# Attention scores of a query block in one PSUM tile: a change to the softmax stage of a two-layer hybrid trunk

## Chip, core and metric

The kernel runs on one core of one Trainium2 chip. The metric is the device time of one execution in microseconds (us). Engines are called PE (TensorE matmuls; PEld its weight loads), DVE (VectorE), ACT (ScalarE), POOL (GpSimd) and SP (SyncE, which issues most DMAs).

## What is computed

The program computes a trunk of two layers over 256 context and 1024 latent tokens (1280 keys) at model width 1024: an S5 state-space mixer with a SwiGLU FFN, then multi-head latent attention with a second FFN. The change lies in the attention alone, which per head is

```
def softmax_attend(q, k, v):
    s = jnp.einsum('bqhd,bkhd->bhqk', q, k).astype(jnp.float32) * (MLA_QK ** -0.5)
    p = jax.nn.softmax(s, axis=-1)
    return jnp.einsum('bhqk,bkhd->bqhd', p.astype(v.dtype), v)
```

There are 16 heads, the queries are the 1024 latent tokens, the keys and values are all 1280 tokens. Work is fp32 throughout: operands are split into a high and a low fp32r part, and a score product is the sum of three matmuls (low by high, high by low, high by high).

## The kernel before

The attention stage is the stretch of `trunk` from the pool `ps4` (L1658) on. A **unit** is one head and one half (512) of the queries; there are 32 (L1684). A unit has four **blocks** of 128 queries and ten **key tiles** of 128 keys.

- `scores_a` (L1697) makes the scores of a block against the first 1024 keys: six matmuls into a two-bank PSUM tile `psS`, of which there are two buffers (L1701), and a `reduce_max` on DVE (L1708).
- `scores_b` (L1711) adds the last 256 keys: three matmuls into the one-bank tile `psE` (one buffer, L1717), a second `reduce_max` on DVE, a DVE `scalar_tensor_tensor` that joins both maxima and scales them by `nsc` (L1722), and two exponentials on ACT, of 256 and of 1024 columns, with the row sums into `rs2` (L1725, L1726). The result is `p`, 128 queries by 1280 keys in SBUF.
- `key_tile` (L1729) transposes four 128x128 pieces of `p` (four blocks, one key tile) on PE into the one-bank tile `psT` (two buffers) and splits the result. For key tiles 1, 4, 6 and 9 (`DIRECT`, L1788) ACT copies PSUM to `ph` and DVE subtracts that from PSUM to give `pl`. For the others ACT copies PSUM to `pf`, DVE casts `pf` to `ph`, and POOL subtracts to give `pl`.
- `pv` (L1763) multiplies a key tile with the values: two matmuls into `psO` (one buffer), and at the tenth a DVE multiplication by the reciprocal row sums.
- `row_sums` (L1747) adds the two halves of `rs2`, takes the reciprocal, transposes it on PE into a `psT` buffer, and sends it through DRAM to be spread over partitions.

The eight PSUM banks are 2x2 for `psS`, 1 for `psE`, 2 for `psT` and 1 for `psO`. The main loop (L1804 to L1830) runs over the units and their ten key tiles. In unit n it transposes and multiplies the `p` of unit n while it makes the scores of unit n+1, one block at key tiles 0, 2, 4 and 6 (`SCORES_AT`): `scores_a`, then `key_tile`, then `scores_b`. `pv` runs five key tiles behind (`LAG`). Before the loop the four blocks of unit 0 are made (the prologue, L1799 to L1802). The order in which each engine runs its instructions is a scheduler's, made from this text and the free buffers; each engine runs its own list in that order, and waits on counters of the other engines.

Of the kernel before, what the change touches and what calls it, by code (L numbers as in the profile page):

```python
# [34 lines left out]
TOK = CTX + SEQ  # L35
# [5 lines left out]
HEADS = 16  # L41
# [142 lines left out]
def trunk(tc, I, out, dbg=None):  # L184
# [20 lines left out]
    V, S, Q, T, D_ = (Engine(*e) for e in zip("VSQTD", (nc.vector, nc.scalar, nc.gpsimd, nc.tensor, nc.sync)))  # L205
# [14 lines left out]
    def copy(o, a):  # L220
        S.activation(o, a, AF.Copy)
# [18 lines left out]
    def pool(name, bufs=1, side="left", space=None):  # L240
        kw = {} if space is None else {"space": space}
        cm = tc.tile_pool(name=name, bufs=bufs, side=side, reuse_waits="tile", **kw)
        p = cm.__enter__()
        opened.append((p, cm))
        return p
# [15 lines left out]
    pp = None  # L261
# [4 lines left out]
    def psG():  # L266
        return psA(4)
# [101 lines left out]
    def const(name, w, p=cp):  # L369
        t = p.tile([128, w], F32, name=name)  # L370
        if p is cp:
            deferred.append((t, I[name]))
        else:
            dma(t, I[name])
        return t
# [7 lines left out]
    ident = const("ident", 128)  # L383
# [54 lines left out]
    def halves(t):  # L438
        return t.rearrange("p (n w) -> p n w", n=2)

    def psN():
        return psB(8).rearrange("p (n w) -> p n w", n=1)
# [90 lines left out]
    pp = pool("ps0", 4, space=PSUM)  # L533
# [607 lines left out]
    def tB():  # L1141
        return hB.tile([128, 2, 640], F32R, name="hb", tag="hb")
# [34 lines left out]
    pp = pool("ps1", 4, space=PSUM)  # L1177
    bgn = norm0_seven(s1, 0, h, psG)
    for c in range(2):
        av = []  # L1180
        for m in range(8):
# [10 lines left out]
            o = tB()  # L1192
# [24 lines left out]
        for m in range(8):  # L1217
            wt = ws.whole(8)
            pt = psG()
# [142 lines left out]
    pp = pool("ps2", 4, space=PSUM)  # L1362
# [4 lines left out]
    pp = ps3 = pool("ps3", 4, space=PSUM)  # L1367
# [5 lines left out]
    sc = pool("sc")  # L1373
    scq = sc.tile([128, 8, HEADS], F32, name="scq")
    nsc = sc.tile([128, 8, HEADS], F32, name="nsc")
# [257 lines left out]
    pp = pool("psq", 4, space=PSUM)  # L1633
# [24 lines left out]
    pp = pool("ps4", 2, space=PSUM)  # L1658
    hA = pool("hA1", 8)
    at = pool("at")  # L1660
    rs2 = at.tile([128, HEADS, 2, 2, 4], F32, name="rs2")
    kv = {}

    def tA1():
# [20 lines left out]
    qts = {}  # L1685
# [9 lines left out]
    open_s = []  # L1695

    def scores_a(n, b):  # L1697

        hd, hf = units[n]
        kt, qt = kv[hd][0], qts[n]  # L1700
        pa = pp.tile([128, 2, 512], F32, name="psS", tag="psS", bufs=2)  # L1701
        qs = slice(b * 128, b * 128 + 128)
        for j, (qp_, kp_) in enumerate(((1, 0), (0, 1), (0, 0))):
            for o, c0 in ((pa[:, 0], 0), (pa[:, 1], 512)):
                T.matmul(o, qt[:, qp_, qs], kt[:, kp_, c0:c0 + 512], start=j == 0, stop=j == 2)
        flat = pa.rearrange("p a b -> p (a b)")
        mx = at.tile([128, 3], F32, name="mx", bufs=4)
        V.reduce_max(mx[:, 0:1], flat, axis=AX.X)  # L1708
        open_s.append((n, b, flat, mx))

    def scores_b():  # L1711

        n, b, flat, mx = open_s.pop()
        hd, hf = units[n]
        kt, qt = kv[hd][0], qts[n]
        i = 4 * hf + b
        pb = pp.tile([128, 256], F32, name="psE", tag="psE", bufs=1)  # L1717
        qs = slice(b * 128, b * 128 + 128)
        for j, (qp_, kp_) in enumerate(((1, 0), (0, 1), (0, 0))):
            T.matmul(pb, qt[:, qp_, qs], kt[:, kp_, 1024:], start=j == 0, stop=j == 2)  # L1720
        V.reduce_max(mx[:, 1:2], pb, axis=AX.X)
        V.scalar_tensor_tensor(mx[:, 2:3], mx[:, 0:1], mx[:, 1:2], nsc[:, i, hd:hd + 1], op0=ALU.max, op1=ALU.mult)  # L1722
        sc = scq[:, i, hd:hd + 1]
        p = at.tile([128, TOK], F32, name="p", bufs=8)
        S.activation(p[:, 1024:], pb, AF.Exp, bias=mx[:, 2:3], scale=sc, accum_out=rs2[:, hd, hf, 1, b:b + 1])  # L1725
        S.activation(p[:, :1024], flat, AF.Exp, bias=mx[:, 2:3], scale=sc, accum_out=rs2[:, hd, hf, 0, b:b + 1])  # L1726
        return p

    def key_tile(ps, k):  # L1729
        tp = pp.tile([128, 512], F32, name="psT", tag="psT", bufs=2)  # L1730
        for b in range(4):
            T.transpose(tp[:, b * 128:b * 128 + 128], ps[b][:, k * 128:k * 128 + 128], ident)
        ph_ = at.tile([128, 512], F32R, name="ph", bufs=6)
        pl_ = at.tile([128, 512], F32R, name="pl", bufs=6)
        if k in DIRECT:
            copy(ph_, tp)
            sub(pl_, tp, ph_.bitcast(F32))
        else:
            pf = at.tile([128, 512], F32, name="pf", bufs=3)
            copy(pf, tp)  # L1740
            V.tensor_copy(ph_, pf)
            sub(pl_, pf, ph_.bitcast(F32), Q)
        return ph_, pl_
# [3 lines left out]
    def row_sums(n):  # L1747

        hd, hf = units[n]
        r4 = at.tile([128, 4], F32, name="r4", bufs=2)  # L1750
        add(r4, rs2[:, hd, hf, 0], rs2[:, hd, hf, 1])
        V.reciprocal(r4, r4)
        pt = pp.tile([128, 512], F32, name="psT", tag="psT", bufs=2)
        T.transpose(pt[0:4, 0:128], r4, ident)
        rt = at.tile([4, 128], F32, name="rt", bufs=2)
        V.tensor_copy(rt, pt[0:4, 0:128])
        dst = rsd[hd:hd + 1, hf * 512:hf * 512 + 512]
        dma(dst.rearrange("a (b p) -> (a b) p", b=4), rt)
        rb = wp.tile([128, 1024], F32, name="rb", tag="wr")
        dma(rb[:, 0:512], dst.to_broadcast([128, 512]))  # L1760
        rbs[n] = rb
# [37 lines left out]
    for b in range(4):  # L1799
        scores_a(0, b)  # L1800
        cur.append(scores_b())
    row_sums(0)  # L1802
    pend = []
    for n in range(NU):  # L1804
        hd, hf = units[n]
        nxt = []
        for k in range(10):
            if n + 1 < NU and k in SCORES_AT:
                scores_a(n + 1, SCORES_AT.index(k))
            if k == 1 and n + 2 < NU:  # L1810
                load_q(n + 2)
            if k == 1 and hf == 0 and hd + 1 < HEADS:
                load_kv(hd + 1)
            if k in (3, 8) and hf == 0 and hd + 1 < HEADS:
                split_k(hd + 1, k // 8)
            if k == 3 and hf == 1 and hd + 1 < HEADS:
                split_v(hd + 1)
            if k == 5 and n + 2 < NU:
                split_q(n + 2)
            if k == 5 and n % 4 == 1 and n > 4:  # L1820
                ot0.append(tA1())
                heads_in(at, n // 4 - 1, 0, ot0[-1])
            pend.append((n, k, key_tile(cur, k)))
            if open_s:
                nxt.append(scores_b())
            if k == 9 and n + 1 < NU:
                row_sums(n + 1)
            if len(pend) > LAG:
                pv(*pend.pop(0))
        cur = nxt  # L1830
# [7 lines left out]
    pp = pool("ps5", 8, space=PSUM)  # L1838
# [33 lines left out]
    for c, (ot, bg, rate) in enumerate(((ot0, second(), 1), (ot1, norm1(s1, 0, h), 2))):  # L1872
        for m in range(8):
# [3 lines left out]
            pt = psN()  # L1877
# [34 lines left out]
```

## Time and profile before

| | us |
|---|---|
| median of 3 runs | 3405.48 (3405.12 to 3406.26) |
| profiled execution | 3405.42 |
| its span, first to last instruction | 3403.6 |
| PE busy in the span | 3181.9 (93%) |
| DVE busy | 2760.2 (81%) |
| ACT busy | 1745.4 (51%) |
| POOL busy | 1032.8 (30%) |
| DVE maxima over psS, 128 of them | 155.6 |
| ACT exponentials over psS, 128 of them | 154.0 |

Busy time counts an instruction from its start to its end. Matmuls overlap, so PE's busy time is not the time that it needs. The granted clock is TensorE's, as a share of its full 2.4 GHz: 1.00, or 0.50 for 1.2 GHz; in a stretch that holds both it is between. "Idle before <- X" names the engine and the tile whose end released an instruction. All helper calls have the line L198, so tiles are told apart by name. The attention stage lies between about 1986 and 2597 us.

### The profile page before, as it was taken

Reading aid. Unit: us, or ns where it says so; the run is one execution under the profiler, and the core shown is the slowest. Engines: PE = TensorE matmul, PEld = TensorE weight load, DVE = VectorE, ACT = ScalarE, POOL = GpSimd, SP = SyncE. Lnnn points to the kernel's source line nnn. Section 1 sums busy time; section 2 is a strip of 40 time slices with the busy share of each in tenths; the row PEclk is TensorE's granted clock in tenths of the full one; section 3 lists DMA queues with packets and bytes.
Section 4 is the critical chain, followed back from the end, with each engine's and each line's share of the span. In section 5 each row is a group of like instructions: output and inputs, shape, how many; then the busy total and the mean of one; then the engine's idle time right before and its main releaser. Section 6 shows DMA issues by size and latency. Waiting matters only on the chain. (4 is left out here: it accounts for less than half of the span.)

```text
span 3403.6 us, 55331 instructions
## 1 busy us (share of the span) xinstructions
PE 3181.9 (93%) x20468; PEld 2922.9 (86%) x20468; DVE 2760.2 (81%) x4640; ACT 1745.4 (51%) x3218; POOL 1032.8 (30%) x812
## 2 busy tenths in 40 slices
PE   6977889999999999999999989899899899999999
PEld 5977789999999999999988767777777799889998
DVE  6878867878888998888867678888885788898887
ACT  5556652424333453344455557777775544454443
POOL 2456510101112121121334345555554421221111
PEclk8988899999999999999999999999999999999999
DMA  7579876552333323323426742222225333233232
GB/s 258 139 162 190 177 196 230 185 180 75 112 101 111 112 81 124 108 67 99 131 95 176 197 122 73 85 67 78 75 70 166 119 104 107 93 120 106 99 107 75
DMA packets 196384, 423.08 MB, mean 124 GB/s; under 512 B 22737, under 2 KB 73873, under 8 KB 195089
## 3 DMA queue, kind: packets, MB, share of 16 engines
q1 hardware_dynamic: 182288, 392.27, 36.1%
q0 software_dynamic: 13824, 27.27, 4.5%
q8 instruction: 162, 2.65, 0.3%
q14 instruction: 110, 0.89, 0.1%
HBM read 326.89 MB, written 53.49 MB: 112 GB/s over the span
## 5 line engine op out<-in xcount | busy, mean ns | idle before, releaser
L198 PE MATMUL psB<-hs,wb 128*128 128x320 f32 (+1 forms) x7392 | 1001.2, 297 | 26.3 <-DVE wb L198 18.6
L198 PEld LDWEIGHTS psB<-hs,wb 128*128 128x128 f32 x7392 | 989.7, 189 | 36.6 <-DVE wb L198 23.2
L198 ACT ACTIVATE wb<-wr 128x512 fp32r<-128x512 f32 (+3 forms) x704 | 404.4, 593 | 448.6 <-PE psB L198 227.6
L198 DVE TENSOR_TENSOR wb<-wr,wb 128x512 fp32r<-128x512 f32 (+3 forms) x704 | 491.9, 709 | 170.1 <-ACT wb L198 169.0
L198 PE MATMUL psB<-hb,wb 128*128 128x320 f32 (+1 forms) x3360 | 602.3, 340 | 12.5 <-ACT hb L198 6.4
L198 PEld LDWEIGHTS psB<-hb,wb 128*128 128x128 f32 x3360 | 544.7, 188 | 65.7 <-ACT hb L198 8.0
L198 POOL TENSOR_TENSOR ws<-wr 128x512 f32<-128x512 f32 x176 | 243.8, 1391 | 1151.4 <-DMA wr<-in_fi 606.0
L198 ACT ACTIVATE wb<-ws 128x512 fp32r<-128x512 f32 x352 | 218.9, 627 | 268.6 <-PE psB L198 195.3
L198 POOL TENSOR_TENSOR pl<-pf,ph 128x512 fp32r<-128x512 f32 x192 | 250.7, 1306 | 259.8 <-DVE ph L198 256.0
L198 DVE TENSOR_TENSOR wb<-ws,wb 128x512 fp32r<-128x512 f32 x352 | 273.8, 782 | 31.2 <-ACT wb L198 29.6
L198 PE MATMUL psA<-ha,wb 128*128 128x320 f32 x1680 | 249.9, 311 | 4.4 <-ACT ha L198 4.4
L198 PEld LDWEIGHTS psA<-ha,wb 128*128 128x128 f32 x1680 | 248.9, 189 | 5.0 <-ACT ha L198 4.6
L198 PE MATMUL psS<-kt,qt 128*128 128x512 f32 x768 | 213.1, 403 | 1.1 <-ACT p L198 1.1
L198 PEld LDWEIGHTS psT<-ident,p 128*128 128x128 f32 x1280 | 147.5, 140 | 72.6 <-issue 20.2
L198 PE MATMUL psT<-ident,p 128*128 128x128 f32 x1280 | 190.1, 275 | 20.3 <-DVE pl L198 17.3
L198 DVE TENSOR_REDUCE mx<-psS 128x1 f32<-128x1024 f32 x128 | 155.6, 1215 | 19.1 <-PE psS L198 18.6
L198 PEld LDWEIGHTS psS<-kt,qt 128*128 128x128 f32 x768 | 139.7, 189 | 29.2 <-ACT p L198 2.1
L198 POOL TENSOR_TENSOR acc<-acc,sq 128x640 f32<-128x640 f32 (+1 forms) x51 | 82.9, 1626 | 249.2 <-ACT sq L198 210.4
L198 ACT ACTIVATE p<-psS,mx,scq 128x1024 f32<-128x1024 f32 x128 | 154.0, 1203 | 0.0
L198 ACT ACTIVATE hb<-sg 128x640 fp32r<-128x640 f32 (+1 forms) x104 | 72.0, 693 | 147.8 <-DVE sg L198 147.4
L198 PE MATMUL psO<-ph,vt 128*128 128x512 f32 x320 | 139.7, 436 | 2.3 <-DVE ph L198 0.4
L198 DVE TENSOR_TENSOR ws<-ws,wr 128x512 f32<-128x512 f32 x88 | 89.2, 1014 | 60.3 <-POOL ws L198 56.6
(339 smaller groups left out, 5569.2 us busy)
## 6 DMA issues: line engine op xcount, KB each, us to landing
wr<-in_fi SPq DMA_DIRECT2D x176, 512.0 KB
wr<-in_mt SPq DMA_DIRECT2D x80, 512.0 KB
wr<-in_swg SPq DMA_DIRECT2D x32, 512.0 KB
wr<-in_fo SPq DMA_DIRECT2D x64, 256.0 KB
wr<-in_fo SPq DMA_DIRECT2D x32, 384.0 KB
ww<-pq POOLq DMA_DIRECT2D x32, 320.0 KB, 4.5
kdr<-big SPq DMA_DIRECT2D x32, 320.0 KB
kt<-kdr SPq DMA_DIRECT2D x16, 640.0 KB
```

What stands on the lines that cost most here:

```text
L198: r = f(*a, **k)
```

## The change

Scores of a block now go into one piece of a PSUM tile `psS` that is allocated once, `[128, 2, 1536]`, six banks: two halves of three banks, used in turn by `turn[0]`. A block uses 1280 of the 1536 columns, two and a half banks. One `reduce_max` and one exponential cover all 1280 columns. The joined maximum falls away; its scaling by `nsc` becomes an ACT `Copy` of 128x1 that the exponential follows. The two spare half banks, columns 1280 to 1535 of both halves, together form a second buffer for the transposes, beside one bank `psT`; `next_t` gives the two in turn, the spare one first. `psO` keeps its bank. `rs2` has one sum for each row, so the addition in `row_sums` is gone.

```
-    rs2 = at.tile([128, HEADS, 2, 2, 4], F32, name="rs2")
+    rs2 = at.tile([128, HEADS, 2, 4], F32, name="rs2")
+    psS = pp.tile([128, 2, 1536], F32, name="psS", tag="psS", bufs=1)
+    psT = (pp.tile([128, 2, 256], F32, name="psT", tag="psT", bufs=1), psS[:, :, TOK:])
+    turn = [0, 0]
+
+    def next_t():
+        turn[1] ^= 1
+        return psT[turn[1]]
...
-        pa = pp.tile([128, 2, 512], F32, name="psS", tag="psS", bufs=2)
+        pa = psS[:, turn[0]]
+        turn[0] ^= 1
...
-            for o, c0 in ((pa[:, 0], 0), (pa[:, 1], 512)):
-                T.matmul(o, qt[:, qp_, qs], kt[:, kp_, c0:c0 + 512], start=j == 0, stop=j == 2)
...
+            for c0 in (0, 512, 1024):
+                c = slice(c0, min(c0 + 512, TOK))
+                T.matmul(pa[:, c], qt[:, qp_, qs], kt[:, kp_, c], start=j == 0, stop=j == 2)
+        mx = at.tile([128, 2], F32, name="mx", bufs=4)
+        V.reduce_max(mx[:, 0:1], pa[:, :TOK], axis=AX.X)
+        open_s.append((n, b, pa[:, :TOK], mx))
...
-            T.matmul(pb, qt[:, qp_, qs], kt[:, kp_, 1024:], start=j == 0, stop=j == 2)
-        V.reduce_max(mx[:, 1:2], pb, axis=AX.X)
-        V.scalar_tensor_tensor(mx[:, 2:3], mx[:, 0:1], mx[:, 1:2], nsc[:, i, hd:hd + 1], op0=ALU.max, op1=ALU.mult)
...
-        S.activation(p[:, 1024:], pb, AF.Exp, bias=mx[:, 2:3], scale=sc, accum_out=rs2[:, hd, hf, 1, b:b + 1])
-        S.activation(p[:, :1024], flat, AF.Exp, bias=mx[:, 2:3], scale=sc, accum_out=rs2[:, hd, hf, 0, b:b + 1])
+        S.activation(mx[:, 1:2], mx[:, 0:1], AF.Copy, scale=nsc[:, i, hd:hd + 1])
+        S.activation(p, pa, AF.Exp, bias=mx[:, 1:2], scale=scq[:, i, hd:hd + 1], accum_out=rs2[:, hd, hf, b:b + 1])
...
-        tp = pp.tile([128, 512], F32, name="psT", tag="psT", bufs=2)
+        tp = next_t()
...
-            copy(ph_, tp)
-            sub(pl_, tp, ph_.bitcast(F32))
+            copy(halves(ph_), tp)
+            sub(halves(pl_), tp, halves(ph_.bitcast(F32)))
...
-            copy(pf, tp)
+            copy(halves(pf), tp)
...
-        add(r4, rs2[:, hd, hf, 0], rs2[:, hd, hf, 1])
-        V.reciprocal(r4, r4)
-        pt = pp.tile([128, 512], F32, name="psT", tag="psT", bufs=2)
-        T.transpose(pt[0:4, 0:128], r4, ident)
+        V.reciprocal(r4, rs2[:, hd, hf])
+        pt = next_t()
+        T.transpose(pt[0:4, 0, 0:128], r4, ident)
```

How the order on the engines moves is shown at three places. The first is PE in the prologue, at the scores of the first two blocks of unit 0, before any transpose into `psS`. Before:

```order
L198 MATMUL psS<-kt,qt 128x512 x2
L198 MATMUL psE<-kt,qt 128x256 [waits PE_49,Activation_49]
L198 MATMUL psE<-kt,qt 128x256 x2
L198 MATMUL psS<-kt,qt 128x512 x6
L198 MATMUL psE<-kt,qt 128x256 [waits Activation_49]
```

Now:

```order
L198 MATMUL psS<-kt,qt 128x512 x2
L198 MATMUL psS<-kt,qt 128x256
L198 MATMUL psS<-kt,qt 128x512 [waits Activation_49]
L198 MATMUL psS<-kt,qt 128x512
L198 MATMUL psS<-kt,qt 128x256
```

Before, the second block's six matmuls on `psS` follow without a wait. Now the second block's first matmul waits for ACT, though it writes the other half of `psS`; the count that it waits for is the one that the exponential of the first block sets.

The second place is PE in the main loop, around one block of scores in a unit whose odd key tiles use the spare half banks. Before, a piece of the loop read:

```order
L198 MATMUL psE<-kt,qt 128x256 [waits Activation_49]
L198 MATMUL psE<-kt,qt 128x256 x2
L198 MATMUL psO<-ph,vt 128x512
L198 MATMUL psO<-pl,vt 128x512 [waits Pool_49]
L198 MATMUL psO<-ph,vt 128x512
L198 MATMUL psO<-pl,vt 128x512
L198 MATMUL psT<-ident,p 128x128 [waits DVE_49,PE_49]
L198 MATMUL psT<-ident,p 128x128 x3
L198 MATMUL psS<-kt,qt 128x512 [waits Activation_49]
L198 MATMUL psS<-kt,qt 128x512 x5
```

Now:

```order
L198 MATMUL psS<-ident,p 128x128 [waits Activation_49]
L198 MATMUL psS<-ident,p 128x128 x3
L198 MATMUL psS<-kt,qt 128x512 [waits Activation_49]
L198 MATMUL psS<-kt,qt 128x512
L198 MATMUL psS<-kt,qt 128x256
L198 MATMUL psS<-kt,qt 128x512 x2
L198 MATMUL psS<-kt,qt 128x256
L198 MATMUL psS<-kt,qt 128x512 x2
L198 MATMUL psS<-kt,qt 128x256
L198 MATMUL psT<-ident,p 128x128 [waits DVE_49]
L198 MATMUL psT<-ident,p 128x128 x3
```

Before, the wait on `psS` was for the exponential two blocks back, which had the same buffer. Now the transposes into `psS` wait for the exponential of the block before, and the scores wait for the copy of those transposes. In the units between (spare half banks at the even key tiles) the transposes wait for the block's maximum on DVE, and the next scores for its exponential.

The third place is DVE and ACT in such a unit between, from the maximum of its second block to the exponential of its third (numbers are kept to tell the tiles apart; `mx_22468` and `p_22479` are the third block's, `pf_22453` and `pf_22493` are copies of its key tiles 3 and 5, `ph_22474` of key tile 4). DVE now:

```order
L198 TENSOR_REDUCE mx_22428<-psS_20211 128x1 [waits PE_49]
L198 CAST ph_22434<-pf_22436 128x512 [waits DVE_49,Activation_49]
L198 CAST ph_22451<-pf_22453 128x512 [waits Activation_49]
L198 TENSOR_REDUCE mx_22468<-psS_20211 128x1 [waits PE_49]
L198 CAST ph_22491<-pf_22493 128x512 [waits DVE_49,Activation_49]
L198 TENSOR_TENSOR pl_22475<-psS_20211,ph_22474 128x512 [waits Activation_49,Pool_49]
```

ACT now:

```order
L198 ACTIVATE pf_22493<-psT_20212 128x512 [waits PE_49]
L198 ACTIVATE mx_22468<-mx_22468,nsc_17580 128x1 [waits DVE_49]
L198 ACTIVATE pf_22530<-psT_20212 128x512 [waits PE_49,Pool_49]
L198 ACTIVATE ph_22474<-psS_20211 128x512 [waits PE_49]
L198 ACTIVATE p_22479,rs2_20210<-psS_20211,mx_22468,scq_17579 128x1280 [waits DVE_49]
```

The cast of key tile 3 stands ahead of the third block's maximum, and two copies with the subtraction `pl_22475` ahead of its exponential.

## Rows read from the trace of the kernel before

**Rows 1.** The page, part 1: busy time of each engine.

```profile
PE 3181.9 (93%) x20468; PEld 2922.9 (86%) x20468; DVE 2760.2 (81%) x4640; ACT 1745.4 (51%) x3218; POOL 1032.8 (30%) x812
```

**Rows 2.** Busy time by stretch: prologue, loop, tail; then granted clock, DMA share, GB/s.

```profile
1986.20:2006.70 20.50, 13.20 (x55) 9.78 (x54) 13.71 (x26) 11.21 (x23) 5.04 (x3) 0.83 0.50 145
2006.70:2581.70 575.00, 523.69 (x2988) 413.65 (x2988) 485.22 (x846) 422.57 (x870) 328.39 (x241) 1.00 0.22 72
2581.70:2597.00 15.30, 13.18 (x73) 9.63 (x72) 10.89 (x17) 7.47 (x15) 10.66 (x9) 1.00 0.44 155
```

**Rows 3.** Instructions on psT: ns min/median/max, first and last start.

```profile
L198 ACT ACTIVATE pf<-psT x192: 577/599/632, 2007.4 to 2591.0; 128x512 f32<-128x512 f32 x192
L198 DVE TENSOR_TENSOR pl<-psT,ph x128: 669/681/694, 2010.3 to 2593.5; 128x512 fp32r<-128x512 f32 x128
L198 PE MATMUL psT<-ident,r x32: 269/271/272, 2006.7 to 2581.7; 128*4 128x128 f32 x32
L198 DVE COPY rt<-psT x32: 269/274/280, 2007.1 to 2582.1; 4x128 f32<-4x128 f32 x32
```

**Rows 4.** Waits in the loop: who for whom, total us, times, longest.

```profile
ACT p L198 <- DVE mx L198: 81.0, 73, 2.7
...
PE psE L198 <- ACT p L198: 26.5, 28, 1.2
...
DVE mx L198 <- PE psS L198: 14.6, 17, 1.0
```

**Rows 5.** Instructions on psS, then on psE: ns min/median/max.

```profile
L198 DVE TENSOR_REDUCE mx<-psS x128: 1205/1212/1227, 1991.7 to 2576.6; 128x1 f32<-128x1024 f32 x128
...
L198 DVE TENSOR_REDUCE mx<-psE x128: 402/410/426, 1992.8 to 2577.8; 128x1 f32<-128x256 f32 x128
```

**Rows 6.** Timeline of the loop: start, us, engine, instruction, [idle before].

```profile
2300.53 1.52 PE L198 MATMUL psS<-kt,qt 128*128 128x512 f32 x6
...
2301.89 0.42 PEld L198 LDWEIGHTS psE<-kt,qt 128*128 128x128 f32 x3
...
2302.09 1.23 DVE L198 TENSOR_REDUCE mx<-psS 128x1 f32<-128x1024 f32 x1
...
2315.75 1.29 POOL L198 TENSOR_TENSOR pl<-pf,ph 128x512 fp32r<-128x512 f32 x1 [1.03 <-DVE ph L198]
...
2316.40 0.60 PE L198 MATMUL psT<-ident,p 128*128 128x128 f32 x4
...
2317.94 0.42 DVE L198 CAST ph<-pf 128x512 fp32r<-128x512 f32 x1
```

**Rows 7.** Timeline of the prologue, same columns.

```profile
1986.65 0.22 ACT L198 ACTIVATE scr<-scq 128x24 f32<-128x24 f32 x1
...
1988.12 1.55 PE L198 MATMUL psS<-kt,qt 128*128 128x512 f32 x6
...
1994.53 0.56 ACT L198 ACTIVATE p<-psE,mx,scq 128x256 f32<-128x256 f32 x1 [5.10 <-DVE mx L198]
...
1995.09 1.20 ACT L198 ACTIVATE p<-psS,mx,scq 128x1024 f32<-128x1024 f32 x1
...
1995.24 1.01 PE L198 MATMUL psE<-kt,qt 128*128 128x256 f32 x3 [5.57 <-ACT p L198]
...
1996.43 2.85 PE L198 MATMUL psS<-kt,qt 128*128 128x512 f32 x6 [0.18 <-ACT p L198]
```

**Rows 8.** Busy time by stretch around pauses of PE; clock third from last.

```profile
105.00:107.00 2.00, 0.16 (x2) 0.00 (x0) 2.00 (x5) 2.00 (x5) 0.00 (x0) 1.00 0.79 281
108.00:111.00 3.00, 3.00 (x13) 3.00 (x12) 3.00 (x5) 0.00 (x0) 0.00 (x0) 0.51 0.75 199
112.00:115.00 3.00, 3.00 (x22) 3.00 (x22) 3.00 (x7) 0.63 (x1) 0.00 (x0) 1.00 0.19 56
...
2909.00:2911.00 2.00, 0.00 (x0) 0.00 (x0) 1.36 (x3) 0.03 (x1) 0.60 (x1) 1.00 0.00 0
2912.00:2915.00 3.00, 2.18 (x18) 1.98 (x18) 3.00 (x5) 2.72 (x6) 0.90 (x1) 1.00 0.01 3
```

More of the change, by code (lines that the diff above doesn't have):

```diff
@@ L1700, in scores_a @@
         kt, qt = kv[hd][0], qts[n]
-        pa = pp.tile([128, 2, 512], F32, name="psS", tag="psS", bufs=2)
+        pa = psS[:, turn[0]]
+        turn[0] ^= 1
         qs = slice(b * 128, b * 128 + 128)
         for j, (qp_, kp_) in enumerate(((1, 0), (0, 1), (0, 0))):
-            for o, c0 in ((pa[:, 0], 0), (pa[:, 1], 512)):
-                T.matmul(o, qt[:, qp_, qs], kt[:, kp_, c0:c0 + 512], start=j == 0, stop=j == 2)
-        flat = pa.rearrange("p a b -> p (a b)")
-        mx = at.tile([128, 3], F32, name="mx", bufs=4)
@@ L1708, in scores_a @@
-        V.reduce_max(mx[:, 0:1], flat, axis=AX.X)
-        open_s.append((n, b, flat, mx))
+            for c0 in (0, 512, 1024):
[4 more added lines that the diff above has]
+        open_s.append((n, b, pa[:, :TOK], mx))
     def scores_b():
-        n, b, flat, mx = open_s.pop()
+        n, b, pa, mx = open_s.pop()
@@ L1714, in scores_b @@
         hd, hf = units[n]
-        kt, qt = kv[hd][0], qts[n]
         i = 4 * hf + b
-        pb = pp.tile([128, 256], F32, name="psE", tag="psE", bufs=1)
-        qs = slice(b * 128, b * 128 + 128)
-        for j, (qp_, kp_) in enumerate(((1, 0), (0, 1), (0, 0))):
-            T.matmul(pb, qt[:, qp_, qs], kt[:, kp_, 1024:], start=j == 0, stop=j == 2)
-        V.reduce_max(mx[:, 1:2], pb, axis=AX.X)
-        V.scalar_tensor_tensor(mx[:, 2:3], mx[:, 0:1], mx[:, 1:2], nsc[:, i, hd:hd + 1], op0=ALU.max, op1=ALU.mult)
@@ L1723, in scores_b @@
-        sc = scq[:, i, hd:hd + 1]
+        S.activation(mx[:, 1:2], mx[:, 0:1], AF.Copy, scale=nsc[:, i, hd:hd + 1])
         p = at.tile([128, TOK], F32, name="p", bufs=8)
-        S.activation(p[:, 1024:], pb, AF.Exp, bias=mx[:, 2:3], scale=sc, accum_out=rs2[:, hd, hf, 1, b:b + 1])
-        S.activation(p[:, :1024], flat, AF.Exp, bias=mx[:, 2:3], scale=sc, accum_out=rs2[:, hd, hf, 0, b:b + 1])
+        S.activation(p, pa, AF.Exp, bias=mx[:, 1:2], scale=scq[:, i, hd:hd + 1], accum_out=rs2[:, hd, hf, b:b + 1])
@@ L1727, in scores_b @@
         return p
     def key_tile(ps, k):
-        tp = pp.tile([128, 512], F32, name="psT", tag="psT", bufs=2)
+        tp = next_t()
         for b in range(4):
-            T.transpose(tp[:, b * 128:b * 128 + 128], ps[b][:, k * 128:k * 128 + 128], ident)
+            T.transpose(tp[:, b // 2, b % 2 * 128:b % 2 * 128 + 128], ps[b][:, k * 128:k * 128 + 128], ident)
         ph_ = at.tile([128, 512], F32R, name="ph", bufs=6)
@@ L1750, in row_sums @@
         r4 = at.tile([128, 4], F32, name="r4", bufs=2)
-        add(r4, rs2[:, hd, hf, 0], rs2[:, hd, hf, 1])
-        V.reciprocal(r4, r4)
-        pt = pp.tile([128, 512], F32, name="psT", tag="psT", bufs=2)
-        T.transpose(pt[0:4, 0:128], r4, ident)
+        V.reciprocal(r4, rs2[:, hd, hf])
+        pt = next_t()
+        T.transpose(pt[0:4, 0, 0:128], r4, ident)
         rt = at.tile([4, 128], F32, name="rt", bufs=2)
-        V.tensor_copy(rt, pt[0:4, 0:128])
+        V.tensor_copy(rt, pt[0:4, 0, 0:128])
         dst = rsd[hd:hd + 1, hf * 512:hf * 512 + 512]
```

## The prediction, as put on record before the changed kernel ran

> **What bounds the kernel now.** I read the busy times of the page first. TensorE is busy 93% of the span, VectorE 81%, ScalarE 51% [rows 1]; that is an average, and the change touches one stage. So next comes the busy time by stretch [rows 2]. The transposes of the row sums come once in each unit, 32 of them from 2006.7 to 2581.7 us [rows 3]: 31 periods of the loop in 575.0 us, 18.55 us each. In that stretch TensorE is busy 523.7 us (91%) at clock 1.00, VectorE 485.2 (84%) and ScalarE 422.6 (73%). In a period TensorE so has 16.9 us of work, the rest is pauses. The list of waits says what the pauses are [rows 4]: TensorE waits for an exponential 28 times, always at the single buffer psE, 26.5 us in all. No wait of TensorE on the two psS buffers stands near the top: the scores of a block run beside the maximum and the exponential of the block before. ScalarE does wait for maxima, 81.0 us, but it has slack. The stage is bound by TensorE's own work with small pauses, and it stays so only while a block's chain (scores, maximum, exponential) overlaps its neighbours'.
>
> **The change, part by part.** The work itself gets less. A maximum takes 1.212 us for 1024 columns and 0.410 for 256 [rows 5], 1.044 ns a column, so 1.48 for 1280; VectorE loses that 0.410, the joining instruction and the addition of the row sums, and gains 0.27. ScalarE loses one fixed start of an exponential and gains a small copy, bounded by its 128x24 instruction, 0.22 us [rows 7]. TensorE has the same nine matmuls and four transposes as before. None of this is worth more than the pauses of TensorE: at most 18.55 - 16.9 = 1.65 us in a period.
>
> What decides is the order. It shows every access to psS, by any engine and in either half, behind the one before it: the second block's scores wait for the first block's exponential already in the prologue, where nothing is transposed yet; in the loop scores, maximum, exponential, the transposes into the spare half banks and the reads of these follow one another. So the loop's period becomes the length of that chain. I add it up, with 0.05 us for each step from one engine to the next (scores that start at 2300.53 and take 1.52 end at 2302.05, the maximum starts at 2302.09 [rows 6]):
>
> - Scores: six matmuls 1.52, and three of 256 columns 0.42 [rows 6]: 1.94, with the step 1.99.
> - Maximum: 1.48, with the step 1.53.
> - Copy of 128x1: 0.22, with the step 0.27.
> - Exponential to the matmul that it releases: 1.34 us for 1024 columns (1995.09 to 1996.43), 0.71 for 256 (1994.53 to 1995.24) [rows 7], so 0.21 more for 1280: 1.55.
> - A block: 5.34.
> - A trip through the spare half banks: four transposes 0.60 [rows 6], ScalarE's copy 0.60 [rows 3], two steps: 1.30. For a direct key tile VectorE's subtraction, 0.68 [rows 3], and a step come on top: 2.03.
>
> Eleven tiles are taken in a unit, so the spare half banks get key tiles 1, 3, 5, 7, 9 in one unit, and 0, 2, 4, 6, 8 and the row sums in the next. The first kind has four blocks, three plain and two direct trips: 21.36 + 3.90 + 4.06 = **29.3 us**. In the second kind the trip lies between maximum and exponential and hides the small copy: a block is 1.99 + 1.53 + 0.65 + 0.60 + 1.55 = 6.32, with a direct tile 0.78 more, 7.10. Two of each, a plain trip of 1.30 and the row sums (0.27 on TensorE and 0.27 on VectorE [rows 3], two steps: 0.65): **28.8 us**.
>
> Then I followed both units through the four queues, since each engine keeps its order, and found what holds the chain up. First kind: at the first block a copy of a psT tile stands ahead of the exponential, 0.6; at the end of the unit the next scores stand behind two value matmuls that wait for POOL's subtractions, 1.29 us each [rows 6], one after the other, some 1.5. Together 2.1: **31.4**. Second kind: value matmuls that wait for POOL ahead of the second and third scores, 0.55 and 0.5. At the third block the maximum stands behind the cast of key tile 3 (0.42 [rows 6]), and that behind a transpose queued after the scores and its copy, so it starts 1.5 late; then two copies, the direct copy and its subtraction stand ahead of the exponential, 2.1 more than the trip alone. The fourth block has 0.2. Together 4.85: **33.6**. The mean is 32.5 us at full clock.
>
> The **clock** is a further term. A pause of TensorE from about 105.2 to 107.7 us, between dense work, is followed by clock 0.51, and full clock is back by 112; one from 2909.0 to 2911.6 leaves it at 1.00 [rows 8]. In the new chain TensorE pauses 2 to 2.8 us while maximum and exponential run, once for each block. A block's scores at half clock take 2.85 us for six matmuls against 1.55, and 1.01 for three against 0.60 where the clock is full [rows 6, 7]; with the loads beside them I take 1.65 us more. The trace bounds this term at 0 and at 4 x 1.65 = 6.6 us a unit. I take one block in three, 2.2 us, nearer the lower end, since pauses of this length have gone both ways and the dense stretch of each block gives the clock back. The values of a tile are now read as two runs of 256 columns; no row shows that, and a second fixed start, at most the 0.35 us that the exponentials' durations leave at zero columns, would add up to 1.7 us a unit in the five trips. I take 0, because the copy's row is of the same size, and keep 1.7 for the upper end.
>
> The sum: 32.5 + 2.2 = 34.7 us a period, 16.15 more than 18.55; 31 x 16.15 = 501. In the prologue three blocks come one after the other, and the first scores after the long pause run at half clock: its end moves by some 6 us. The tail has no scores and keeps its 15.3 us [rows 2]. Against the profiled execution, 3405.4 us (span 3403.6 and 1.8 around it; 0.06 us from the median of the runs): 3405.4 + 501 + 6 = **3912 us**.
>
> **The rivals.** *The bare chain.* If the hold-ups fall out differently on the chip and the clock stays up, only the chain counts, (29.3 + 28.8) / 2 = 29.05: 31 x 10.5 + 6 = 332 more, **3737 us**. For it: the queues were followed by hand, from mean durations. Against it: the queues' order is fixed, and the largest hold-ups are of the chain's own engines.
>
> *Half clock throughout.* Every block pays 1.65: 32.5 + 6.6 = 39.1, 31 x 20.55 + 6 = 643 more, **4048 us**. For it: TensorE would be busy about half of the time. Against it: the prologue's 1995 to 1999 us end at full clock again after about 4 us of work.
>
> *Waits only where a bank is shared.* The two halves of psS lie in different banks, three each. If the scores of a block did not in fact have to wait for the exponential in the other half (the counter long reached), then in the units of the second kind the exponential, 1.55 a block, leaves the chain; the transposes of the first kind span both halves and keep it. That gives 33.6 - 6.2 = 27.4, a mean of 29.4 and 31.6 with the clock: **3816 us**. The Trainium skill, in PSUM — Partial Sum Buffer, under PSUM bank collisions raise a hardware error, states that two engines on different banks do not collide and that guards belong to bank and quadrant; by that rule alone the order would need no such wait, and this is the time that it would give. Against it: the order has the wait, in the prologue too.
>
> *Faster.* If the transposes and value matmuls filled all the time in which a chain runs, so that a second block was always under way, TensorE's 16.9 us would be the period: 31 x 1.65 = 51 less, **3354 us**. It decides from the point at which the next scores start before the exponential ends. For it speaks the lighter VectorE. Against it: in the order nothing of the next block stands ahead of that wait, and between two waits TensorE has one tile of transposes and four value matmuls, some 1.4 us against about 3.3 of maximum, copy and exponential.
>
> **How the numbers follow.** My forecast (serial chain, hold-ups, some clock) gets 0.79, half clock throughout 0.08, the bare chain 0.07, the bank rule 0.04, faster 0.02. The range reaches from 3790, which takes in the bank rule's time and a third of the hold-ups gone, to 4050, which takes in half clock and the split reads; the bare chain and the faster case stay outside. A change under 0.2% (7 us) is about what a measurement of this kernel can't tell from none. Faster by more than that 0.02, within it 0.01, slower 0.97.
>
> **What would show it.** Right: in the loop TensorE waits for ScalarE and VectorE ahead of psS in every block; the row sums' transposes come every 33 to 36 us; TensorE's busy share in the loop falls to about half, the clock to 0.7 to 0.9; VectorE and ScalarE have less busy time and are idle more. The maximum takes 1.48 us. Wrong: scores of a block that start while the exponential before them still runs; a period under 29 us; a clock that stays at 1.00 or at 0.5; or stretches outside the attention that change.

## The result, and the profile after

The changed kernel takes 3980.42 us (median of 4 runs, 3964.42 to 3982.94), the kernel before 3405.87 beside it: a ratio of 1.167 (95% interval 1.165 to 1.170). The prediction, 3912 us with a range of 3790 to 4050, holds the time; it was 68 us short of the median. The profiled execution took 3964.42 us with a span of 3962.6; the steps below are compared with that one, where the forecast was 52 us short.

The page's part 1 of the changed kernel, against [rows 1]: the other engines' work is less or at most 6.2 us more (ACT), yet PE is busy 264 us longer with as many instructions, since much of its work ran at half clock.

```profile
PE 3445.7 (87%) x20468; PEld 3072.9 (78%) x20468; DVE 2680.1 (68%) x4352; ACT 1751.6 (44%) x3090; POOL 1027.3 (26%) x812
```

Busy time by stretch, columns as in [rows 2]: from the first scores to the first row sums, then the loop, then the last unit's transposes and values up to the last subtraction from psT.

```profile
1978.50:2009.10 30.60, 12.76 (x41) 9.77 (x41) 10.66 (x12) 10.23 (x17) 4.39 (x3) 0.76 0.32 95
2009.10:3130.10 1121.00, 780.03 (x2999) 556.25 (x2999) 409.95 (x569) 427.63 (x747) 320.42 (x241) 0.80 0.11 37
...
3130.10:3149.10 19.00, 15.34 (x64) 10.79 (x62) 9.81 (x14) 7.73 (x15) 11.25 (x9) 0.77 0.36 119
```

The loop, measured again between the first and the last transpose of row sums, takes 1121.0 us in place of 575.0: 36.16 us a period in place of 18.55. That is 546.0 of the 559.0 us between the two profiled executions. The first row sums come 2.4 us later, and what follows the last ones is 10.6 us longer. DVE is busy 410.0 us in the loop, 75 less than before, and the clock is 0.80 in place of 1.00.

Instructions on the tiles of the change (ns min/median/max, first and last start), beside [rows 3, 5]:

```profile
L198 DVE TENSOR_REDUCE mx<-psS x128: 1483/1492/1493, 1983.4 to 3123.9; 128x1 f32<-128x1280 f32 x128
L198 ACT ACTIVATE mx<-mx,nsc x128: 294/295/299, 1984.9 to 3125.5; 128x1 f32<-128x1 f32 x128
L198 ACT ACTIVATE p<-psS,mx,scq x128: 1412/1417/1424, 1986.5 to 3125.8; 128x1280 f32<-128x1280 f32 x128
...
L198 ACT ACTIVATE pf<-psS x96: 597/597/598, 2026.9 to 3144.9; 128x512 f32<-128x512 f32 x96
...
L198 DVE TENSOR_TENSOR pl<-psS,ph x64: 669/692/693, 2018.2 to 3143.4; 128x512 fp32r<-128x512 f32 x64
...
L198 PE MATMUL psS<-ident,r x16: 373/373/418, 2009.1 to 3095.1; 128*4 128x128 f32 x16
...
L198 PE MATMUL psT<-ident,r x16: 271/415/415, 2045.0 to 3130.1; 128*4 128x128 f32 x16
```

One maximum and one exponential cost what their columns say. Reading a tile as two runs of 256 columns costs next to nothing: 597 ns against the 599 of [rows 3] for the copy, 692 against 681 for the subtraction.

The waits in the loop (who for whom, total us, times, longest), beside [rows 4]:

```profile
ACT mx L198 <- DVE mx L198: 443.4, 108, 7.3
DVE mx L198 <- PE psS L198: 356.5, 124, 5.6
...
PEld psS L198 <- ACT p L198: 162.3, 94, 3.2
...
PE psS L198 <- ACT p L198: 120.4, 91, 2.8
...
PEld psS L198 <- ACT pf L198: 67.6, 63, 1.4
PEld psS L198 <- DVE mx L198: 66.4, 45, 2.0
```

TensorE's matmuls now wait for an exponential ahead of psS 91 times in 31 units. VectorE waits for scores 124 times, that is for every block, where it had waited 17 times. Each of these engines waits for the one before it in the chain.

The timeline shows one link of that chain, at the end of the loop where the clock is full (start, us, engine, instruction, [idle before]):

```profile
3121.88 2.02 PE L198 MATMUL psS<-kt,qt 128*128 128x512 f32 x9 [0.75 <-ACT pf L198]
...
3123.93 1.49 DVE L198 TENSOR_REDUCE mx<-psS 128x1 f32<-128x1280 f32 x1 [0.84 <-PE psS L198]
...
3125.46 0.29 ACT L198 ACTIVATE mx<-mx,nsc 128x1 f32<-128x1 f32 x1 [3.15 <-DVE mx L198]
3125.79 1.42 ACT L198 ACTIVATE p<-psS,mx,scq 128x1280 f32<-128x1280 f32 x1
...
3127.35 0.69 PE L198 MATMUL psS<-ident,p 128*128 128x128 f32 x4 [2.09 <-ACT p L198]
3128.14 0.60 ACT L198 ACTIVATE pf<-psS 128x512 f32<-128x512 f32 x1 [0.84 <-PE psS L198]
...
3128.79 1.11 PE L198 MATMUL psS<-ident,p 128*128 128x128 f32 x4 [0.75 <-ACT pf L198]
```

From the scores' start to the transposes that the exponential releases: 5.47 us (5.34 forecast). From there to the next use of psS: 1.44 (1.30 forecast). No instruction here runs on psS beside another engine's, and that holds for the whole trace of the change: no matmul into either half overlaps a maximum, an exponential, a copy or a subtraction that reads the tile. The transposes at 3128.79 take 1.11 us in place of 0.69: after TensorE's pause of 2.09 us the granted clock fell to 0.50 at 3127.8, while the transposes before them ran.

The clock is seen unit by unit. Busy time by stretch, two units of the second kind (row sums in psT to row sums in psS), then two of the first; the clock stands third from last, and each stretch begins and ends where the weights of a row sums' transpose are loaded:

```profile
2260.90:2300.20 39.30, 27.66 (x101) 19.12 (x100) 12.58 (x19) 14.70 (x27) 14.54 (x11) 0.76 0.09 28
2335.50:2371.20 35.70, 23.82 (x101) 16.07 (x100) 12.26 (x18) 13.95 (x26) 11.69 (x9) 0.88 0.10 30
2371.20:2406.70 35.50, 24.72 (x96) 18.45 (x96) 14.05 (x20) 13.26 (x24) 8.04 (x7) 0.78 0.14 50
2514.90:2547.90 33.00, 22.60 (x96) 16.71 (x97) 14.19 (x20) 13.42 (x24) 8.18 (x7) 0.86 0.17 54
```

A clock of 0.86 over 33.0 us is 2 x 0.14 x 33.0 = 9.2 us at 1.2 GHz. From transpose to transpose, the first kind takes 35.0 us in the mean (16 units) and the second 37.4 (15 units); by the weight loads, which come up to 0.4 us earlier, it is 34.7 and 37.7. A straight line through a unit's length against its us at half clock comes to 31.1 us without any for the first kind and to 32.3 for the second. So the chain at full clock is estimated at some 31.7 us, and the clock's cost at some 4.5. That is an extrapolation, since every unit has 8 us or more at half clock; the runs below bear on it.

### The profile page after: what moved, and what is told of

The parts are those of the page before. It is cut to its first block, busy times and chain, and to the rows that moved or that the text cites. A ratio compares the mean times of both kernels' runs of the same rounds, so it can differ in the third digit from the quotient of the medians.

```text
span 3962.6 us, 55017 instructions
## 1 busy us (share of the span) xinstructions
PE 3445.7 (87%) x20468; PEld 3072.9 (78%) x20468; DVE 2680.1 (68%) x4352; ACT 1751.6 (44%) x3090; POOL 1027.3 (26%) x812
## 3 DMA queue, kind: packets, MB, share of 16 engines
q1 hardware_dynamic: 182288, 392.27, 31.1%
## 5 line engine op out<-in xcount | busy, mean ns | idle before, releaser
L198 PE MATMUL psB<-hs,wb 128*128 128x320 f32 (+1 forms) x7392 | 1004.8, 298 | 22.0 <-DVE wb L198 14.5
L198 PEld LDWEIGHTS psB<-hs,wb 128*128 128x128 f32 x7392 | 994.1, 190 | 31.4 <-DVE wb L198 19.5
L198 DVE TENSOR_REDUCE mx<-psS 128x1 f32<-128x1280 f32 x128 | 190.9, 1492 | 374.1 <-PE psS L198 368.7
L198 PE MATMUL psS<-kt,qt 128*128 128x512 f32 (+1 forms) x1152 | 353.6, 470 | 52.5 <-ACT pf L198 24.1
L198 PEld LDWEIGHTS psS<-kt,qt 128*128 128x128 f32 x1152 | 273.7, 265 | 126.8 <-ACT pf L198 33.7
L198 DVE TENSOR_TENSOR wb<-ws,wb 128x512 fp32r<-128x512 f32 x352 | 270.8, 773 | 31.6 <-ACT wb L198 29.9
L198 PE MATMUL psS<-ident,p 128*128 128x128 f32 x640 | 121.4, 319 | 174.1 <-ACT p L198 111.8
L198 PEld LDWEIGHTS psS<-ident,p 128*128 128x128 f32 x640 | 77.7, 156 | 231.5 <-ACT p L198 147.2
L198 ACT ACTIVATE mx<-mx,nsc 128x1 f32<-128x1 f32 x128 | 37.7, 295 | 464.1 <-DVE mx L198 463.6
L198 PE MATMUL psO<-ph,vt 128*128 128x512 f32 x320 | 170.7, 533 | 60.8 <-DVE ph L198 38.2
L198 DVE CAST ph<-pf 128x512 fp32r<-128x512 f32 x192 | 83.5, 435 | 201.2 <-ACT pf L198 199.7
L198 PE MATMUL psO<-pl,vt 128*128 128x512 f32 x320 | 160.3, 501 | 42.1 <-POOL pl L198 34.1
L198 ACT ACTIVATE p<-psS,mx,scq 128x1280 f32<-128x1280 f32 x128 | 181.4, 1417 | 19.3 <-DVE pl L198 17.5
```

What stands on the lines that cost most here:

```text
L198: r = f(*a, **k)
```

## The experiments

Times are medians, in us, with the ratio to the kernel before on the same chip and its 95% interval. "Period" is the loop's time over its 31 units, by the row sums' transposes in the run's trace.

**1. Two separate score tiles, one transpose bank.**

```
-    psS = pp.tile([128, 2, 1536], F32, name="psS", tag="psS", bufs=1)
-    psT = (pp.tile([128, 2, 256], F32, name="psT", tag="psT", bufs=1), psS[:, :, TOK:])
+    psT = pp.tile([128, 2, 256], F32, name="psT", tag="psT", bufs=1)
...
-        pa = psS[:, turn[0]]
-        turn[0] ^= 1
+        pa = pp.tile([128, 1536], F32, name="psS", tag="psS", bufs=2)
```

`next_t` always gives psT here.

> The change with its two halves of psS as two separate three-bank tiles, the spare half banks unused, all transposes through the one bank psT; one maximum and one exponential a block stay. Theory (the cost is that all accesses to the one psS tile stand one behind the other): scores of the next block run beside maximum and exponential of the one before, the loop's period falls from 36.2 to 19 to 23 us, the clock in the loop to 0.98 or more, the time to 3420 to 3550 us. What is then left over the kernel before is the single transpose bank, whose ten trips are six of 1.30 and four of 2.03 us and the row sums, 16.6 us a unit. Rival (the cost is the long pieces themselves, the maximum of 1.49 us followed by an exponential of 1.42, or the exponential behind a small ACT copy): the period stays above 30 us, the time above 3790.

Measured: 3621.05 (1.0625, 1.0609 to 1.0641), 359 below the change. Period 25.2 us. The loop by stretch, columns as in [rows 2]:

```profile
2002.70:2783.80 781.10, 617.76 (x2998) 432.15 (x2997) 445.38 (x570) 428.33 (x747) 322.29 (x242) 0.97 0.16 53
```

The waits in that loop, at the transpose bank and at the score tiles:

```profile
ACT pf L198 <- PE psT L198: 203.2, 151, 2.9
...
DVE mx L198 <- PE psS L198: 61.0, 62, 1.7
...
PE psS L198 <- ACT p L198: 12.4, 31, 1.0
```

TensorE's 120.4 us of waiting for exponentials shrink to 12.4, and the clock is back at 0.97. The rival of the long pieces is out, as it stood (30 us or more). But the period is 2.2 us above the upper end: a part of the cost was not in my theory. Run 5 finds it.

**2. One score tile, spare half banks unused.**

```
-        turn[1] ^= 1
-        return psT[turn[1]]
+        return psT[0]
```

> The change with its one psS tile, but all transposes go through the one bank psT; the spare half banks stay unused. Theory (a serial chain of scores, maximum, copy and exponential, to which the trips through the spare half banks are added): the chain of a unit is four blocks of 5.4 us, 21.6, and with a little half clock the period is 22 to 26 us, the time 3520 to 3640 us; waits of TensorE on psS for ScalarE's exponential stay, those for the copy of spare tiles go. Rival (the spare half banks alone are the cost, and the order between the two halves of psS costs nothing): 19 to 21 us a period, 3420 to 3480, as with two separate tiles.

Measured: 3674.92 (1.0782, 1.0766 to 1.0799); period 26.7, just over the range. Using the spare half banks thus costs 9.5 of the change's 36.2 us, net of what a second transpose buffer saves, and with the clock that it brings. Three of this run's units by stretch:

```profile
2146.00:2172.80 26.80, 21.02 (x99) 14.95 (x99) 12.93 (x19) 13.88 (x24) 11.10 (x8) 0.94 0.13 40
...
2517.80:2546.10 28.30, 21.01 (x97) 14.96 (x97) 13.56 (x19) 14.60 (x26) 13.24 (x10) 0.94 0.12 37
2546.10:2571.00 24.90, 19.70 (x97) 13.80 (x98) 12.97 (x20) 13.99 (x25) 9.81 (x7) 1.00 0.22 72
```

Units at clock 1.00 take 24.8 to 25.3 us (10 of them), and with two tiles 24.7 to 25.4 (20 of 22). So without the trips the serial chain of the blocks, 4 x 5.47 = 21.9 us, lies under another bound of about 25; my theory for this run named the wrong bound. Run 5 shows which it is.

**3. TensorE kept busy.** Ahead of a transposition into the spare half banks:

```
+        if tp is psT[1]:
+            for _ in range(6):
+                T.matmul(psT[0].rearrange("p a b -> p (a b)"), fill[:, 0:128], fill, start=True, stop=True)
```

> The change, with six matmuls of 512 columns added ahead of each transposition into the spare half banks, on constant data and into the other transpose bank; their result is not used. They fill part of TensorE's pauses and add up to about 1.4 us of work to a trip. Theory (half clock is worth 3 to 4 us of the 36.2 us period): the loop's clock rises from 0.80 to 0.95 or more, nine score matmuls take 2.0 us always, and the period is 33 to 35 us, less what the added work delays, so 3860 to 3930 us. Rival (my hold-ups were too small and the clock costs little): the clock rises and the period stays at 36 us or goes above it, 3960 us or more.

Measured: 3830.71 (1.1239, 1.1217 to 1.1262), 150 below the change although TensorE does more. Period 31.84, below the range. By stretch, a unit of the second kind and one of the first, both at clock 1.00:

```profile
2939.50:2969.20 29.70, 26.05 (x130) 19.26 (x128) 11.29 (x17) 12.10 (x22) 7.75 (x7) 1.00 0.08 27
2969.20:3000.20 31.00, 24.93 (x125) 19.05 (x126) 13.06 (x19) 13.28 (x23) 7.90 (x6) 1.00 0.05 18
```

The loop's clock is 0.95. The one unit of the first kind at full clock takes 31.0 us (31.2 from transpose to transpose), near the 31.1 of the line through the change's units. The second kind, all 15 units at clock 1.00, takes 29.5 to 30.8 from transpose to transpose, under the 32.3 of its line, so either that line is off or the added matmuls changed more than the clock. The period is 4.3 us shorter; the nine score matmuls, whose length shows the clock directly, account for 2.1 of that. How the rest divides between clock and order is not shown, and 4.5 us for the clock stays an estimate.

**4. Spare half banks at the odd key tiles in every unit**, without and with the added matmuls:

```
-        tp = next_t()
+        tp = psT[k % 2]
...
-        pt = next_t()
+        pt = psT[0]
```

Without the added matmuls:

> The change with the spare half banks used at the odd key tiles in every unit (before: odd in one unit, even and the row sums in the next), so that all units are of the first kind. Theory (the two kinds cost what the trace of the change shows, 35.0 and 37.4 us): a period of 35 us, 1.2 us less than the mean now, 31 x 1.2 = 36 us less in all, about 3928 beside the profiled 3964. Rival (the lengths depend on how the two kinds follow one another, or on the clock): no change within 10 us, or more.

With them, placed as in run 3:

> Spare half banks at the odd key tiles in every unit, which alone gave 37.4 us a period at clock 0.77, and six unused matmuls ahead of each transposition into them. Theory (that run was longer than the change through its clock alone): clock 0.93 or more, 31 to 33.5 us a period as the units of this kind with added matmuls show (31.0 at clock 1.00, 33.5 at 0.92), 3795 to 3875 us. Rival (a unit of this kind is longer after one of its own kind, whatever the clock): clock up, period still 35.5 us or more.

Measured: 4001.77 (1.1736, 1.1716 to 1.1755) without, a miss: slower than the change, where some 36 us less were expected. With the matmuls 3831.18 (1.1246, 1.1213 to 1.1279). The loop by stretch, without:

```profile
2012.40:3171.40 1159.00, 795.86 (x3003) 582.73 (x3001) 423.29 (x569) 433.44 (x746) 323.52 (x241) 0.77 0.11 36
```

And with:

```profile
2009.70:2988.50 978.80, 802.94 (x3933) 613.54 (x3932) 409.12 (x570) 431.80 (x746) 330.48 (x242) 0.97 0.13 43
```

37.4 us a period at clock 0.77, 31.6 at 0.97, and the 15 units at clock 1.00 take 30.4 to 31.3, 30.8 in the mean. Kept to one kind, the kernel had settled into a rhythm in which nearly every unit has the same 17.1 us at half clock, where the change's units of this kind mostly have 14.5; at full clock the kind is as short here as in run 3. The first and the third block's scores of one such unit:

```profile
2424.47 1.99 PE L198 MATMUL psS<-kt,qt 128*128 128x512 f32 x9
...
2440.61 3.57 PE L198 MATMUL psS<-kt,qt 128*128 128x512 f32 x9 [0.69 <-ACT pf L198]
```

In nearly every unit the first block's scores take 1.98 to 2.25 us and the other three's 3.3 to 3.6. The scores so account for 3.7 of the 5.8 us between the two runs. That 37.4 - 30.8 = 6.6 us is also what the prediction had for four blocks at half clock is chance: only three blocks pay, and by 1.3 to 1.6 us each.

**5. The kernel before with one transpose bank.**

```
-        tp = pp.tile([128, 512], F32, name="psT", tag="psT", bufs=2)
+        tp = pp.tile([128, 512], F32, name="psT", tag="psT", bufs=1)
...
-        pt = pp.tile([128, 512], F32, name="psT", tag="psT", bufs=2)
+        pt = pp.tile([128, 512], F32, name="psT", tag="psT", bufs=1)
```

> The kernel before with one bank psT instead of two for the transposes; nothing else is changed. Theory (what two separate score tiles had left over the kernel before, 25.2 against 18.55 us a period, is the lost transpose bank): 24 to 25.5 us a period, 3575 to 3625 us. Rival (it is the long maximum and exponential or the small ACT copy): 21 us a period or less, 3480 us or less.

Measured: 3613.47 (1.0611, 1.0581 to 1.0641), within the range. The loop by stretch:

```profile
2009.40:2790.70 781.30, 614.76 (x2992) 445.14 (x2990) 494.73 (x847) 434.82 (x870) 333.75 (x242) 0.93 0.17 53
```

781.3 us, against 781.1 with long pieces and two score tiles (run 1). So the lost bank explains most or all of what run 1 had left over the kernel before. The two loops are not at the same clock, though (0.93 and 0.97): units at clock 1.00 take 24.1 us in the mean here (8 units, 23.1 to 25.6) and 25.0 in run 1 (22 units). That the long maximum and exponential and the small ACT copy cost up to about 1 us a period is not excluded.

**6. Two score tiles, and the spare half banks of both in use**, each half copied by itself:

```
+    psS = [pp.tile([128, 1536], F32, name=f"psS{i}", tag=f"psS{i}", bufs=1) for i in range(2)]
+    one = pp.tile([128, 2, 256], F32, name="psT", tag="psT", bufs=1)
+    psT = ([one[:, 0], one[:, 1]], [t[:, TOK:] for t in psS])
...
-        pa = psS[:, turn[0]]
+        pa = psS[turn[0]]
...
```

The rest of the edit, left out here, fits the copies, subtractions and transposes to the two pieces.

> Two separate three-bank tiles for psS, and the spare half banks of both as second transpose buffer, each half read and copied by itself (copies and subtractions of 256 columns). So an access waits only for the accesses to its own three banks. Theory (the change pays for waits across the two halves, and the transposes through spare banks still tie both tiles to one another): 26 to 29.5 us a period at nearly full clock, 3640 to 3750 us, 200 us or more below the change. Rival one (the trips through the spare half banks alone make the chain, however the tiles are cut): 31.5 us or more, 3810 us or more. Rival two (once cut, the spare half banks are as good as the second bank before): 22 us or less, 3520 us or less.

Measured: 3572.91 (1.0482, 1.0455 to 1.0510), 407 below the change and between the theory and its second rival; period 23.8. Two units by stretch, second kind, then first:

```profile
2449.20:2475.80 26.60, 21.72 (x102) 15.19 (x100) 14.59 (x23) 15.55 (x34) 15.27 (x11) 0.94 0.13 40
2475.80:2497.00 21.20, 18.01 (x95) 13.11 (x95) 12.63 (x19) 12.88 (x26) 7.98 (x6) 1.00 0.26 85
```

In the second of them, scores of a block run during the maximum and the exponential of the block before:

```profile
2489.12 1.49 DVE L198 TENSOR_REDUCE mx<-psS 128x1 f32<-128x1280 f32 x1 [0.21 <-PE psS L198]
...
2489.83 2.01 PE L198 MATMUL psS<-kt,qt 128*128 128x512 f32 x9
...
2490.97 1.42 ACT L198 ACTIVATE p<-psS,mx,scq 128x1280 f32<-128x1280 f32 x1
```

Same banks and same scores, maxima and exponentials as the change; only what counts as one tile is cut finer (and copies and subtractions of the spare half banks come in two). That is worth 12.3 us a period, clock included.

**7. Looking for a version that wins.** On run 1, no direct key tiles (`DIRECT = ()`). On run 6, the spare half banks at the odd key tiles in every unit; then, on that, `DIRECT = (0, 4, 6, 8)`; then, on that, `LAG = 7` with eight buffers for `ph` and `pl`.

> Two separate score tiles and one transpose bank, with no direct key tiles: ScalarE copies each transposed tile out, VectorE casts it, POOL subtracts; the bank is free after the copy. Theory (the single bank's round of trips is the bound): its round falls from 16.6 to 10 x 1.30 + 0.65 = 13.7 us a unit, the period from 25.2 by about four times VectorE's 0.69 and what queued behind it, to 19 to 22.5 us, 3425 to 3530 us; under 3405 if TensorE's own 16.9 us come within 1.6 us. Rival (POOL, with 10.4 + 4 x 1.28 = 15.5 us a unit, is then late for the value matmuls): 24 us or more, 3575 us or more.

> Two separate score tiles and the spare half banks of both, now at the odd key tiles in every unit and the row sums in psT. With the alternation of the change, units with odd spare tiles took 21.2 us and the others 26.6. Theory (the kind decides, since at the odd tiles no trip stands between a maximum and its exponential): 21 to 22 us a period, 3485 to 3520 us. Rival (a unit of this kind is short because the one before it was long and left work done): 23 us or more, 3550 us or more.

> As the run with odd spare tiles in every unit, but the direct key tiles are 0, 4, 6 and 8 in place of 1, 4, 6 and 9, so that no tile in the spare half banks is direct and each is free after ScalarE's copy. Theory (the trips through the spare half banks still hold up scores): 0.69 us and a step less for two trips, 0.5 to 2 us a period less than with the direct tiles among them, 19.5 to 21 us, 3440 to 3490 us. Rival (the bound is now elsewhere, the one psT bank or POOL): no change within 0.4 us a period, 12 us in all, or more.

> As the run with direct key tiles 0, 4, 6 and 8, and the value matmuls seven key tiles behind in place of five, with eight buffers for each part. Theory (what is left are TensorE's waits for POOL's subtractions ahead of value matmuls, 83.8 and 57.4 us over 34 periods, partly at once, in the run with alternating spare tiles): 1 to 2.5 us a period less than at five, 3380 to 3450 us. Rival (TensorE then waits for the transposes' banks instead): within 0.4 us a period of the run at five.

(In the last one "34 periods" should read 31.) Measured, in this order: 3570.29 (1.0485, 1.0465 to 1.0505), 3658.66 (1.0741, 1.0712 to 1.0770), 3497.58 (1.0266, 1.0239 to 1.0294), 3496.65 (1.0264, 1.0237 to 1.0290). The first lies between the two expectations: without direct tiles the period is 1.6 us shorter, 23.6. Its waits in part of the loop name what is late next:

```profile
ACT pf L198 <- PE psT L198: 257.9, 162, 6.1
...
PEld psO L198 <- POOL pl L198: 177.3, 198, 2.6
```

The second is a miss and on its rival's side: 26.9 us a period at clock 0.89, so the kind alone does not make a unit short. How much of its length its clock explains, and why that fell so far, stays open. The third is 8 us above the upper end of its range, but by chance: against the run before it the period falls by 5.5 us, where 0.5 to 2 were expected, and how that divides between the direct tiles and the clock is not shown. Its loop has clock 0.99 and 21.4 us a period:

```profile
1998.80:2662.20 663.40, 562.71 (x3000) 424.49 (x3000) 445.93 (x570) 441.34 (x904) 324.73 (x242) 0.99 0.19 63
```

The fourth changes nothing, as its rival had it: the value matmuls' waits for POOL are not the end of the chain. None beats the kernel before; the best is 2.6% slower.

## Why the prediction was right, and where it was off

**Direction and mechanism.** The step that decided, that every access to psS stands behind the one before it in either half, is what the chip does: the timeline's link, the 124 and 91 waits, the absence of any overlap on psS in the whole trace, and the pair of run 6 and the change show it. What the change saves (75 us of VectorE in the loop) was worth nothing, as forecast. Runs 1 and 2 add a limit that the prediction did not state: the order across the two halves costs little by itself (26.7 us a period against 25.2), because the single transpose bank then bounds the loop at about 25 us; it costs much together with the trips through the spare half banks. The time comes out 52 us short of the profiled execution: 45 in the loop and 10.6 in the tail, less 3.6 that the prologue was put too long.

**The bare chain** was slightly short. A block is 5.47 for 5.34 and a trip 1.44 for 1.30. Nine score matmuls take 2.02 us, not 1.94, since the 0.42 for the last three was read off a row of weight loads. The 128x1 copy on ACT costs 0.295 us, not the 0.22 taken from a 128x24 instruction; the rest is steps between engines of 0.05 to 0.19 where 0.05 was put everywhere.

**The hold-ups** were too long. They and the chain were to give 31.4 and 33.6 us; the lines through the change's units give 31.1 and 32.3, and run 3 has a unit of the first kind at 31.2. With the longer bare chain, the first kind has about half a us of hold-up in place of 2.1. Mean 31.7 for 32.5.

**The clock** is the term that was mis-sized: 2.2 us a period forecast, some 4.5 by the estimate above. "One block in three" (1.33 of a unit's four) at 1.65 us each was wrong in its count. Of the loop's 124 blocks, the nine score matmuls of 47 took 1.90 to 2.03 us and those of 77 took 2.29 to 3.57. That is 2.5 blocks a unit, each 1.20 us longer than the 2.01 of full clock: 3.0 us a period in the scores alone. The price of 1.65 was near the most that a block paid (3.57 - 2.01 = 1.56). The other 1.5 us of the estimate has no term in the prediction; transposes at half clock (mostly 1.06 to 1.12 us for four, in place of 0.60 to 0.69) stand in the chain too. The pauses were also not as forecast: of over 2 us there are 28 in the 124 blocks, of over 1 us 113. I had weighed the two pauses of [rows 8], one of which cost nothing; why that one did, and why 47 blocks kept the full clock, no run shows. The two errors partly cancel: -0.8 and +2.3 make 36.2 for 34.7, 45 us over the loop. That the forecast is no further off is partly luck.

**Prologue and tail.** From the first scores to the first row sums takes 30.6 us, against 20.4 before: 10 us more where 6 were forecast; its end moves by 2.4 us only. That the first scores start 7.8 us earlier, at 1978.5, isn't put down to the change: among the profiles of this study they start between 1976.9 and 1988.8. The tail was costed at nothing because it "has no scores", and took 10.6 us more than before. 7.2 of it lie in the last unit's transposes and values, at clock 0.77 (19.0 us to the last subtraction from psT at 3149.1, against 11.8 at clock 1.00 before). How much of that is the clock and how much the order of the transposes is not shown. The other 3.4 come later; from there to 3200 us the clock is 0.94.

**The rivals.** Half clock throughout came true nowhere: even in run 4, at clock 0.77, the first block's scores ran at or near full clock. The bare chain and the faster case are excluded by the time. Two of the signs did not come out as stated: the period is 36.2 us, just over 33 to 36, and TensorE is busy 70% of the loop (780 of 1121 us), not half, since matmuls at half clock take longer. "Waits only where a bank is shared" lies inside the range by its time, but the 91 waits and the missing overlap exclude it for the change. The finer cut of run 6 comes nearest to that case: 23.8 us a period, well under the 29.4 that I had worked out for it, since cutting the tile also lets the transposes of one half go ahead while the other half's exponential runs. The Trainium skill, in PSUM — Partial Sum Buffer, under PSUM bank collisions raise a hardware error, asks for guards by bank and quadrant. Run 6 orders accesses by three-bank tile, which keeps to that rule, and at 23.8 us a period it shows that the change's order across both halves is stricter than the rule needs.

**What the change costs, by runs.** Per period: 18.55 before; 25.2 with one transpose bank and two separate score tiles (runs 1 and 5; 26.7 with one score tile, run 2; 23.6 without direct tiles, run 7); 23.8 with the spare half banks in cut tiles as a second one (run 6); 36.2 with both halves in one tile (the change), of which some 4.5 is clock by estimate. The second transpose bank that the long score tile displaces was worth 6.7 us a period, and the spare half banks, which are free only when no scores stand beside them, give back 1.4 of that (3.8 with other direct tiles and at the odd key tiles in every unit).

## What to carry to other kernels

Before merging buffers into one tile, look at how the order treats the tile: if accesses to any part wait for accesses to every other part, two halves are not two buffers, and the pipeline between engines becomes a chain. Count what a bank does before giving it away; here a transpose bank was worth far more than one long reduction. Where a change puts regular pauses of 1 to 3 us on TensorE, read from the nearest trace how the clock took them, and price the half clock for all of TensorE's work in the chain, transposes too; here 77 of 124 blocks paid, and the work behind the loop ran at clock 0.77 as well.

## What the runs showed of the hardware

- Adding TensorE work made a kernel faster: six matmuls (mostly 1.5 to 1.7 us together) ahead of a transposition took the loop from 36.2 to 31.8 us a period, and with odd spare tiles from 37.4 to 31.6, while the granted clock rose from 0.80 and 0.77 to 0.95 and 0.97. The score matmuls, shorter at the higher clock, are 2.1 and 3.7 us a period of that.
- The time at half clock does not fix a unit's length: in run 2, units at clock 1.00 take 24.8 to 25.3 us, and units at 0.94, with the same 3.4 us at half clock, 26.4 to 28.8.
- The clock keeps to a rhythm: with all units of one kind (run 4), most of them had the same 17 us at half clock; with two kinds in turn (the change) it varied from unit to unit (8 to 20 us).
- Scores that ran during a maximum and an exponential on another three-bank tile (run 6) took 2.01 us, as long as alone.
- A 128x1 copy on ACT takes 0.295 us, a maximum over 1280 PSUM columns 1.492 and an exponential over them 1.417, with 0.192 us for reading out its row sum.
